# A Strassen embedding computed between the pieces of the output projection, kept in DRAM, and a rewritten last stage

## The chip, the cores and the metric

The kernel runs on one core of one Trainium2 chip. The metric is the device time of one execution in microseconds (us), and the time shown for a kernel is the median of several executions. The core has five engines with queues of their own: TensorE (PE, the matmuls), VectorE (DVE), ScalarE (ACT), GpSimd (POOL) and SyncE (SP). Transfers between DRAM and the on-chip memory SBUF are issued from the SP queue and from the POOL queue, each in its own order; an issue that has to wait holds back every later issue of its queue. Matmuls write to banks of 128 x 512 f32.

## What is computed

```python
hn  = rmsnorm(x, norm_g)                       # x: 512 x 2048, f32
y   = swa_mixer(hn, w_in, w_out, sinks, rel_bias)   # sliding-window attention,
                                               # ends with (out * silu(gate)) @ w_out
x   = x + y
emb = p @ ple_proj                             # 512 x 256 by 256 x 2048
g   = sigmoid(rmsnorm(x, ple_norm) @ ple_gate) # 2048 x 2048 weights
x   = x + emb * g
return rmsnorm(x, final_g)
```

`emb` depends on the inputs `p` and `ple_proj` alone, so it may be computed anywhere before its use in the last line but one.

## The kernel before

**Arithmetic.** Every f32 product is three matmuls in a reduced f32 form: each operand is split into a high part (a cast) and a low part (what the cast left), and `mm3` issues high x high (L126), high x low (L127) and low x high (L128).

**Strassen's scheme.** The two large products with `w_out` and with `ple_gate` (2048 x 2048 each) are computed by Strassen's scheme on quarters. Seven products replace eight. Six of them run in the order 1, 7, 6, 5, 3, 4 (`ORDER_OUT`, `ORDER_PLE`), and one is split once more into seven "small" products. A place in the program is written (p, jj, m): product p, column half jj (0 or 1), piece m (0 to 3). One such piece is a 512 KB block of weights, 128 x 1024, and 12 matmuls of 512 columns into a pair of banks. A small product takes one piece with 6 matmuls at a time; the table `SMALL` says behind which (p, jj, m) each stands.

**The life of a weight piece.** `Pieces` numbers all pieces in the order of use. A piece is loaded by SP (`braw`, L747), some pieces ahead; then ScalarE casts it to `bhi` (L754) and VectorE subtracts that from it to get `blo` (L755). Both go into three buffers each, so the cast of piece n can start only when the last matmul of piece n-3 is done, and the subtraction only when the cast is done. The split of a piece is asked for two pieces ahead of its use. Pieces of the far stretch (from product 6 of `w_out` to the end of that stage) are loaded into eight shared 512 KB rooms (tag "grown"); sums of weights for some products are formed beforehand in DRAM (`sum_weights`) or in these rooms by POOL transfers that add.

**The stages.** Norm, input projection and attention come first (to about 450 us), then the output projection, whose results are added to `x1s` from the banks, then the norm before the gate with transposes (`hT`), then the gate's product, sigmoid and embedding, then the final norm and the stores.

**The embedding before.** It is the direct product: eight "proj" pieces of 512 KB in the gate stage (table `EMBEDS`), split like all pieces, and for each 128 rows x 512 columns six matmuls into a bank of their own (`embed`, bank `e`). The operand p is loaded and split once (`pT` into `pTh`, `pTl`). In the last stage (product 4 of `ple_gate`) the function `block` issues the 24 matmuls of one block of 128 rows and then the block's embedding matmuls; the last block is cut into 288 and 224 columns, `lower` and `upper`. The generator `gated` then takes the sigmoid on ScalarE (L1223), multiplies it by the embedding bank on VectorE (L1225), adds it to x (L1229 on VectorE or by a POOL transfer that adds), and squares for the norm. For the first three of the five last blocks VectorE subtracts the Strassen term kept in `s2` after the matmuls (L1399); for the last two ScalarE writes -`s2` into the bank first and the matmuls add on top.

**What sets the order.** The instructions of PE and SP stand in the order in which they are written, all through. Those of DVE, ACT and POOL are ordered by a scheduler up to the second product of the gate stage, and from there on as they are written too.

## Time and profile before

| | |
|---|---|
| time, median of 3 runs | 789.53 us (789.5 to 790.0) |
| the profiled execution | 789.45 us |
| its span from first to last instruction | 787.7 us |
| mean granted PE clock | 0.996 |
| PE busy | 778.7 us, 99% of the span |
| DVE, ACT, POOL busy | 607.9, 507.0, 139.6 us |
| the last stage, 751.75 to 779.60 us | PE 27.85 of 27.85 us busy |

The 1.75 us between the profiled execution's time and its span lie around the span, where no instruction is recorded. Rows of the timeline give start and length in us; rows of groups give the count, then busy time in us and the mean of one in ns.

### The profile page before, as it was taken

What the parts mean: (1) busy time and instruction counts of PE and PEld (TensorE: products, weight loads), DVE (VectorE), ACT (ScalarE), POOL (GpSimd) and SP (SyncE); (2) the same over time, 40 slices, a digit from 0 to 9 for tenths busy, and PEclk for the clock granted to TensorE, in tenths of its full rate; (3) what the DMA queues carried; (4) which work ended last, traced back from release to release, by engine and by line L of the source; (5) the groups of instructions that cost most, each with busy time, mean ns of one, the idle gap of its engine ahead of it and who ended that gap; (6) DMA issues with size and microseconds to landing.
All of it is one profiled execution on the core that took longest, in us unless ns stands there. A gap on an engine that the chain in (4) does not pass through costs nothing. (4 is left out here: it accounts for less than half of the span.)

```text
span 787.7 us, 11098 instructions
## 1 busy us (share of the span) xinstructions
PE 778.7 (99%) x3726; PEld 651.8 (83%) x3726; DVE 607.9 (77%) x1037; ACT 507.0 (64%) x1064; POOL 139.6 (18%) x258
## 2 busy tenths in 40 slices
PE   9999999999999999999999999999999999999995
PEld 8888888888888888888888888888888888888885
DVE  4547697876877688777777898778879589877896
ACT  6743576666767576766666754456689666656953
POOL 0201423132223323122222200000000022202000
PEclk9999999999999999999999999999999999999998
DMA  9978999999999989999997489667873899979723
GB/s 346 294 206 298 194 274 298 292 280 269 280 275 258 271 232 309 256 289 263 282 258 197 136 320 383 207 209 238 270 265 108 292 290 262 247 239 251 208 86 129
DMA packets 47817, 198.07 MB, mean 251 GB/s; under 512 B 7104, under 2 KB 8128, under 8 KB 42000
## 3 DMA queue, kind: packets, MB, share of 16 engines
q1 hardware_dynamic: 38736, 151.95, 55.7%
q0 software_dynamic: 9024, 45.41, 30.0%
q8 instruction: 29, 0.48, 0.3%
q14 instruction: 28, 0.23, 0.1%
HBM read 189.16 MB, written 71.35 MB: 331 GB/s over the span
## 5 line engine op out<-in xcount | busy, mean ns | idle before, releaser
L755 DVE TENSOR_TENSOR blo<-braw,bhi 128x1024 fp32r<-128x1024 f32 x108 | 131.5, 1222 | 37.3 <-ACT bhi L754 36.4
L754 ACT CAST bhi<-braw 128x1024 fp32r<-128x1024 f32 x108 | 113.4, 1051 | 55.9 <-PE o L128 25.9
L126 PE MATMUL gps<-xh,whi 128*128 128x512 f32 x256 | 100.0, 390 | 0.0
L127 PE MATMUL gps<-xl,whi 128*128 128x512 f32 x256 | 99.9, 390 | 0.0
L128 PE MATMUL gps<-xh,wlo 128*128 128x512 f32 x256 | 99.7, 390 | 0.0
L126 PE MATMUL qps<-xh,whi 128*128 128x512 f32 x224 | 87.8, 392 | 0.0
L127 PE MATMUL qps<-xl,whi 128*128 128x512 f32 x224 | 87.4, 390 | 0.0
L128 PE MATMUL qps<-xh,wlo 128*128 128x512 f32 x224 | 87.3, 390 | 0.0
L110 DVE TENSOR_TENSOR wlo<-wraw,whi 128x1024 fp32r<-128x1024 f32 x60 | 73.5, 1227 | 2.8 <-ACT whi L109 2.7
L570 POOL TENSOR_SCALAR_AFFINE_SELECT own<-r 64x512 fp32r<-64x512 f32 (+1 forms) x48 | 32.5, 677 | 242.9 <-DVE r L560 237.2
L126 PE MATMUL o<-bhi,fho 128*128 128x512 f32 x192 | 74.8, 390 | 0.0
L128 PE MATMUL o<-bhi,flo 128*128 128x512 f32 x192 | 74.8, 389 | 0.0
L127 PE MATMUL o<-blo,fho 128*128 128x512 f32 x192 | 74.7, 389 | 0.0
L556 ACT CAST r<-pt 128x256 fp32r<-128x256 f32 x64 | 23.9, 374 | 68.8 <-PE pt L551 68.6
L109 ACT CAST whi<-wraw 128x1024 fp32r<-128x1024 f32 x60 | 62.3, 1040 | 4.6 <-issue 4.1
L126 PE MATMUL g<-bhi,fhg 128*128 128x512 f32 x160 | 62.7, 392 | 0.0
L128 PE MATMUL g<-bhi,flg 128*128 128x512 f32 x160 | 62.3, 389 | 0.0
L127 PE MATMUL g<-blo,fhg 128*128 128x512 f32 x160 | 62.3, 389 | 0.0
L128 PEld LDWEIGHTS gps<-xh,wlo 128*128 128x128 f32 x256 | 48.1, 188 | 10.3
L126 PEld LDWEIGHTS gps<-xh,whi 128*128 128x128 f32 x256 | 48.1, 188 | 9.1
L127 PEld LDWEIGHTS gps<-xl,whi 128*128 128x128 f32 x256 | 48.1, 188 | 8.8
L560 DVE TENSOR_TENSOR r<-pt,r 128x256 fp32r<-128x256 f32 x56 | 23.7, 424 | 41.0 <-ACT r L556 40.3
(244 smaller groups left out, 1789.3 us busy)
## 6 DMA issues: line engine op xcount, KB each, us to landing
wraw<-in_w_gate_in SPq DMA_DIRECT2D x32, 512.0 KB, 8.3
w_out<-in_w_out POOLq DMA_DIRECT2D x32, 512.0 KB, 9.0
braw<-w_out SPq DMA_DIRECT2D x32, 512.0 KB, 4.8
wraw<-in_w_q SPq DMA_DIRECT2D x28, 512.0 KB, 6.6
braw<-in_w_out SPq DMA_DIRECT2D x22, 512.0 KB, 4.1
braw<-in_ple_gate SPq DMA_DIRECT2D x22, 512.0 KB, 5.4
xw<-in_first SPq DMA_DIRECT2D x14, 640.5 KB, 6.7
w_out<-in_w_out SPq DMA_DIRECT2D x16, 512.0 KB, 10.2
```

Source lines behind the costliest of these rows:

```text
L109: nc.scalar.copy(hi, raw)
L110: nc.vector.tensor_sub(lo, raw, hi.bitcast(F32))
L126: nc.tensor.matmul(ps, sh, mh, start=first, stop=False, skip_group_check=more)
L127: nc.tensor.matmul(ps, sh, ml, start=False, stop=False, skip_group_check=more)
L128: nc.tensor.matmul(ps, sl, mh, start=False, stop=last, skip_group_check=more)
L556: nc.scalar.copy(rh, src)
L560: nc.vector.tensor_sub(rl, src, rh.bitcast(F32))
L570: nc.gpsimd.affine_select(out=flat(own), in_=flat(r).bitcast(F32), pattern=[[0, 8], [sign, HB]], compare_op=ALU.is_ge, fill=0.0, base=-HB ...
L754: nc.scalar.copy(hi, raw)
L755: nc.vector.tensor_sub(lo, raw, hi.bitcast(F32))
```

## The change

The embedding leaves the gate stage. A new class `Embedding` computes it by Strassen's scheme: for each column half, seven products of quarter blocks (two blocks of 128 rows each, three matmuls each: 42 matmuls, all 512 wide), in nine slots between pieces of the output projection (`EMBED_AT`). The sums of quarters of p are made on chip (`make_forms`), the sums of quarters of `ple_proj` with 256 KB loads, two VectorE additions and two POOL transfers that add for each column half, in the rooms of s1 and s7; in each slot the sum is split like a weight piece (the pieces of kind "emb" are numbered with the others). Results come out of the banks by ScalarE copies or VectorE additions, partial sums are put back into banks by ScalarE, and eight 512 KB stores on the POOL queue keep the embedding in DRAM (`embeds`). The gate stage reads them back by eight 512 KB loads on SP in place of the "proj" pieces; `gated` multiplies by that tile instead of a bank.

The small products of `w_out` start later, in product 3 instead of product 5, and (4, 1, 0) has two of them in a row. Pieces of the far stretch are loaded at most 5 ahead instead of 6, and a growing sum is asked for 3 pieces after its last use instead of 6.

In the last stage all five blocks start from a bank that ScalarE has filled with -`s2` (`open_bank`), so no subtraction (old L1399) is left. More additions to x go by POOL transfers, the square of block (3, 1)'s lower part is taken on ScalarE, and some rows are scaled on ScalarE (`rows_by_root`), with the gain multiplied on VectorE.

```diff
     SMALL = {
         "w_out": {
-            (5, 0): {1: [1], 3: [1]}, (5, 1): {1: [7], 3: [7]}, (3, 0): {1: [6], 3: [6]}, (3, 1): {1: [2], 3: [2]},
-            (4, 0): {0: [5], 1: [5], 2: [4], 3: [4]}, (4, 1): {0: [3], 1: [3]},
+            (3, 0): {1: [1], 2: [1], 3: [7]}, (3, 1): {0: [7], 1: [6], 2: [6], 3: [2]},
+            (4, 0): {0: [2], 1: [5], 2: [5], 3: [4]}, (4, 1): {0: [4, 3], 1: [3]},
         },
...
                 if n is not None:
-                    self.due.append((i + (2 if self.specs[i][0] == "seed" else 6), n))
+                    self.due.append((i + (2 if self.specs[i][0] == "seed" else 3), n))
                     self.due.sort()
...
-        def add_embeds(of, j):
-            at["e", of] = len(B.specs)
-            B.add("proj", a["ple_proj"].rearrange("(k p) d -> p k d", p=P)[:, :, j * 512 : (j + 1) * 512])
-
...
+                    if nm == "w_out" and (p, jj, m) in EMBED_AT:
+                        at.setdefault("embed", []).append(len(B.specs))
+                        B.add("emb", None)
...
-                for of, j in EMBEDS.get((p, jj), ()) if nm == "ple_gate" else ():
-                    add_embeds(of, j)
         return at
     EMBEDS = {
-        (6, 1): [((1, 0), 0)], (5, 0): [((1, 1), 1), ((5, 0), 2)], (5, 1): [((5, 1), 3)],
-        (3, 0): [((3, 0), 2)], (3, 1): [((3, 1), 3)],
+        (6, 1): [(1, 1)], (5, 0): [(5, 0)], (5, 1): [(5, 1)], (3, 0): [(3, 0)], (3, 1): [(3, 1)],
     }
+
+    EMBED_AT = [
+        (6, 1, 0), (6, 1, 1), (6, 1, 3), (5, 0, 0), (5, 0, 2), (5, 0, 3), (5, 1, 1), (5, 1, 2), (3, 0, 0),
+    ]
...
     small_steps = {
-        (6, 1, 2): 1, (5, 0, 0): 7, (5, 0, 2): 7, (5, 1, 0): 6, (5, 1, 2): 6, (3, 0, 2): 2, (3, 1, 0): 5, (3, 1, 2): 5,
-        (3, 1, 3): 4, (4, 0, 1): 3, (4, 0, 3): 3,
+        (5, 1, 2): 1, (5, 1, 3): 7, (3, 0, 1): 7, (3, 0, 2): 6, (3, 0, 3): 6, (3, 1, 0): 2, (3, 1, 1): 5, (3, 1, 2): 5,
+        (4, 0, 0): 4, (4, 0, 1): 3, (4, 0, 2): 3,
+    }
+
+    embeds = {
+        (c, jj): tc.dram_tile([P, 2, 512], F32, name=f"embeds{c}_{jj}") for c in (1, 5, 3, 4) for jj in range(2)
...
+    class Embedding:
...
+            elif step == "sums0":
+                load(b50, src(2, 1, 0))
+                load(b51, src(1, 1, 1))
+                nc.vector.tensor_add(b30, b4, b31)
+                nc.vector.tensor_add(b21, b30, b1)
+                add(b4, src(1, 1, 0))
+                add(b50, b21)
+                B.base.update(zip(self.at, (b1, self.b2, self.b3, b4, b5)))
...
+        def times(self, q, piece, half, banks, first=False):
+            fh, fl = self.forms[q]
+            (bh, bl) = (v[half] for v in piece)
+            for tb in range(2):
+                mm3(banks[tb], fh[:, blk(tb)], fl[:, blk(tb)], bh, bl, first, True, True)
+
+        def bank_pair(self, name, tag):
+            return [bank(f"{name}{self.done}_{tb}", tag) for tb in range(2)]
+
+        def room(self, c):
+            return late.tile([P, 2, 512], F32, tag="grown", name=f"made{c}_{self.done}", bufs=8)
+
+        def keep(self, c, jj, fill, to=None):
+            to = self.room(c) if to is None else to
+            for tb in range(2):
+                fill(to[:, tb], tb)
+            nc.gpsimd.dma_start(embeds[c, jj], to)
+
+        def slot(self):
+
+            k = self.done
+            jj = 0 if k < 5 else 1
+            piece = B.get(self.at[k])
+            if k == 0:
+                self.left()
+            if k in (4, 8):
+                self.times(4, piece, 0, self.Z)
+                self.keep(4, jj if k == 8 else 0, lambda to, tb: nc.scalar.copy(to, self.Z[tb]))
+            if k in (0, 4):
+                self.X = self.bank_pair("eX", "t")
+                self.times(1, piece, 1 if k else 0, self.X, True)
+                self.O = self.bank_pair("eO", "o")
+                for tb in range(2):
+                    nc.scalar.mul(self.O[tb], self.X[tb], -1.0)
+            elif k in (1, 5):
+                self.times(2, piece, 0, self.O)
+                self.times(6, piece, 1, self.X)
+                self.keep(1, jj, lambda to, tb: nc.scalar.copy(to, self.O[tb]))
+                self.Y = self.bank_pair("eY", "o")
+                for tb in range(2):
+                    nc.scalar.copy(self.Y[tb], self.X[tb])
+            elif k in (2, 6):
+                self.times(7, piece, 0, self.Y)
+                self.times(3, piece, 1, self.X)
+                for tb in range(2):
+                    nc.scalar.copy(self.left_of[:, tb], self.Y[tb])
+                self.upper = self.room(3)
+                for tb in range(2):
+                    nc.scalar.copy(self.upper[:, tb], self.X[tb])
+            elif k in (3, 7):
+                self.W = self.bank_pair("eW", "o")
+                self.times(5, piece, 0, self.W, True)
+                self.keep(5, jj, lambda to, tb: nc.vector.tensor_add(to, self.W[tb], self.left_of[:, tb]))
+                self.keep(3, jj, lambda to, tb: nc.vector.tensor_add(to, self.W[tb], to), self.upper)
+                self.Z = self.bank_pair("eZ", "o")
+                for tb in range(2):
+                    nc.scalar.mul(self.Z[tb], self.left_of[:, tb], -1.0)
+            self.done += 1
+
...
+    embedding = Embedding(at_out["embed"])
+    embed_steps = {
+        (7, 1, 2): "p", (6, 0, 0): "load0", (6, 0, 1): "forms", (6, 0, 2): "sums0", (6, 1, 1): "load1", (6, 1, 2): "load2",
+        (5, 0, 0): "load3", (5, 0, 1): "sums1",
     }
...
+                if (p, jj, m) in EMBED_AT:
+                    embedding.slot()
...
-    pT = wpool.tile([P, WE], F32, tag="wraw", name="pT").rearrange("p (k t) -> p k t", k=2)
-    nc.sync.dma_start(pT, a["pT"])
-    nc.scalar.copy(pTh, pT)
-    nc.vector.tensor_sub(pTl, pT, pTh.bitcast(F32))
     done = {t: 0 for t in range(NB)}
-    def embed(t, w, tag, c=slice(0, 512)):
-        e_ps = bank(f"e{t}_{done[t]}", tag)
-        for k in range(2):
-            mm3(e_ps[:, c], pTh[:, k, blk(t)], pTl[:, k, blk(t)], w[0][k][:, c], w[1][k][:, c], k == 0, k == 1)
-        return e_ps
-
-    def gated(t, j, zin, z, e_ps, c=slice(0, 512), share=1.0):
+    embed_of = {}
+
+    def load_embeds(c, jj):
+        t = embed_of[c, jj] = late.tile([P, 2, 512], F32, tag="e", name=f"e{c}_{jj}", bufs=2)
+        nc.sync.dma_start(t, embeds[c, jj])
+
+    def embeds_for(of, which):
+        return {t: embed_of[of, which][:, t % 2] for t in ((2, 3) if of == 5 else (0, 1))}
+
+    embed_loads = {
+        (6, 0, 3): (1, 0), (6, 1, 1): (1, 1), (5, 0, 1): (5, 0), (5, 1, 1): (5, 1), (3, 0, 1): (3, 0), (3, 1, 1): (3, 1),
+        (3, 1, 3): (4, 0),
+    }
+
+    def gated(t, j, zin, z, e, c=slice(0, 512), share=1.0):
...
-        nc.vector.tensor_mul(z, e_ps[:, c], z)
-        if (t >= 2) == (j >= 2):
+        nc.vector.tensor_mul(z, e[:, c], z)
+        if (t >= 2) == (j >= 2) or (t, j) in ((0, 2), (1, 2), (2, 0)):
+            if t < 2 and j < 2:
+                yield
...
+    opened = {}
+
+    def open_bank(jj, tb, tag, c=slice(0, 512)):
+
+        ps = opened[jj, tb, c.start] = bank(f"open{jj}_{tb}_{c.start}", tag)
+        nc.scalar.mul(ps[:, c], s2[:, jj, tb, c], -1.0)
+
+    opens = {
+        (3, 1, 0): (0, 0, "t"), (3, 1, 1): (1, 0, "t"), (3, 1, 2): (0, 1, "o"), (3, 1, 3): (1, 1, "o", lower),
+    }
...
-    def block(jj, tb, tag, e_tag, c=slice(0, 512), share=1.0, opened_ps=None):
-
-        ps = bank(f"last{jj}_{tb}_{c.start}", tag) if opened_ps is None else opened_ps
+    def block(jj, tb, c=slice(0, 512), share=1.0):
+
+        ps = opened[jj, tb, c.start]
         for k in range(8):
             fh, fl = f[k // 2]
             bh, bl = B.made[at_ple[4, jj][k // 2]]
             mm3(
                 ps[:, c], fh[:, k % 2, blk(tb)], fl[:, k % 2, blk(tb)], bh[k % 2][:, c], bl[k % 2][:, c],
-                k == 0 and opened_ps is None, k == 7, opened_ps is not None,
+                False, k == 7, True,
             )
-        e_ps = embed(2 + tb, w[jj], e_tag, c)
-        z = s2[:, jj, tb, c]
-
-        def opened():
-            if opened_ps is not None:
-                return gated(2 + tb, jj, ps[:, c], z, e_ps, c, share)
-            nc.vector.tensor_sub(z, ps[:, c], z)
-            return gated(2 + tb, jj, z, z, e_ps, c, share)
-
-        return opened
-
-
+        return gated(2 + tb, jj, ps[:, c], s2[:, jj, tb, c], embed_of[4, jj][:, tb], c, share)
...
+    def rows_by_root(t, js):
+        for j in js:
+            nc.scalar.mul(x1[j][:, t, :], x1[j][:, t, :], yn2[:, t : t + 1])
+            store(t, j)
...
-    g = block(0, 1, "p", "o")()
     run(root)
-    next(g)
-    upper_ps = opened_bank(1, 1, "s", upper)
+    for j in (2, 3):
+        by_gain(3, j)
     for j in range(2):
         row(2, j, yn2[:, 2:])
         store(2, j)
-    for j in (2, 3):
-        nc.scalar.mul(x1[j][:, 2, :], x1[j][:, 2, :], yn2[:, 2:])
-        store(2, j)
+    g = block(0, 1)
     next(g)
+    next(g)
+    rows_by_root(2, (2, 3))
     run(g)
     base, yn = (const.tile([P, 1], F32, name=f"{v}_3") for v in ("base", "yn"))
-    g = block(1, 1, "p", "t", lower, opened_ps=lower_ps)()
+    g = block(1, 1, lower)
+    next(g)
     next(g)
     by_gain(3, 0)
-    next(g)
     run(g)
     n = done[3]
-    last = block(1, 1, "s", "o", upper, 1.0 / D, upper_ps)()
+    last = block(1, 1, upper, 1.0 / D)
     next(last)
     nc.vector.tensor_reduce(base, ssq3[:, 3, :n], axis=AX.X, op=ALU.add)
```

TensorE, the end of its program. `open` is the bank of the last 224 columns, `last`/`low` the high and low part of the last weight pieces, `fhg`/`flg` those of the activations, `e` the embedding's bank. Before:

```order
L128 MATMUL open_1_288_7793<-last_7641,flg_10_7475 128x224
L126 MATMUL open_1_288_7793<-last_7641,fhg_11_7501 128x224
L127 MATMUL open_1_288_7793<-low_7645,fhg_11_7501 128x224
L128 MATMUL open_1_288_7793<-last_7641,flg_11_7502 128x224
L126 MATMUL e_4_7868<-bhi_7617,pTh 128x224
L127 MATMUL e_4_7868<-blo_7618,pTh 128x224
L128 MATMUL e_4_7868<-bhi_7617,pTl 128x224
```

And TensorE around the embedding's second slot, behind piece (6, 1, 1) of the output projection, after the change (`o` are that product's banks, `eO` and `eX` the embedding's, `p_high`, `p_low` and `p_rest` parts of p):

```order
L127 MATMUL o_1_1_5134<-blo_5506,fho_01_5280 128x512
L128 MATMUL o_1_1_5134<-bhi_5505,flo_01_5281 128x512
L126 MATMUL eO_0_5539<-bhi_5526,p_high 128x512
L127 MATMUL eO_0_5539<-blo_5527,p_high 128x512
L128 MATMUL eO_0_5539<-bhi_5526,p_low 128x512
L126 MATMUL eO_1_5540<-bhi_5526,p_high 128x512
L127 MATMUL eO_1_5540<-blo_5527,p_high 128x512
L128 MATMUL eO_1_5540<-bhi_5526,p_low 128x512
```

The matmuls of the bank `e` are gone from the gate stage, and 84 others stand in the nine slots; in all PE's program is 18 rows shorter.

VectorE around the subtraction that makes the second form of the transposed activations (`hT`, 128 x 4 x 256) while the last pieces of the output projection are split. Before, the splits there are of pieces 58 and 59:

```order
L755 TENSOR_TENSOR blo_6206<-braw_6108,bhi_6205 128x1024
L1054 TENSOR_TENSOR x1s<-smallo_6154,x1s 128x512
L755 TENSOR_TENSOR blo_6218<-braw_6120,bhi_6217 128x1024
L863 SCALAR_TENSOR_TENSOR flg_01_6275<-hT_6050,fhg_01_6274 128x512
L855 TENSOR_TENSOR hT_6050<-hT_6050 128x4x256
L755 TENSOR_TENSOR blo_6240<-braw_6155,bhi_6239 128x1024
```

After, those of pieces 65, 66 and 67:

```order
L1049 TENSOR_TENSOR x1s<-o_0_1_6244,x1s 128x512
L756 TENSOR_TENSOR blo_6425<-braw_6339,bhi_6424 128x1024
L756 TENSOR_TENSOR blo_6439<-braw_6375,bhi_6438 128x1024
L861 SCALAR_TENSOR_TENSOR flg_01_6508<-hT_6265,fhg_01_6507 128x512
L853 TENSOR_TENSOR hT_6265<-hT_6265 128x4x256
L756 TENSOR_TENSOR blo_6463<-braw_6387,bhi_6462 128x1024
```

ScalarE there after the change, from the cast of piece 65 (`bhi_6424`) to that of piece 66, with four evacuations of transposes between:

```order
L755 CAST bhi_6424<-braw_6339 128x1024
L1036 ACTIVATE hT_6265<-tp_0_6407,pn 128x256 x2
L1036 ACTIVATE hT_6316<-tp_0_6414,pn 128x256 x2
L755 CAST bhi_6438<-braw_6375 128x1024
L1019 ACTIVATE s_5037,ssq_5034<-x1s 128x512
```

On VectorE the rows are the same as before, but the piece whose low part stands behind the subtraction is now piece (4, 1, 1), whose two predecessors on PE are small products of 6 matmuls; before, one of 6 and one of 12 stood there.

GpSimd's queue after the change, from the second set of weight sums (`s`, in the rooms of s1 and s7) to the norm before the gate (`rstd`); `made` is a 512 KB room that holds one quarter column of the embedding:

```order
L1240 DMA embeds_0_5043<-made_2_5646 128x1024
L1188 DMA s_5038<-in_ple_proj 128x512
L1189 DMA s_5038<-s_5036 128x512
L1240 DMA embeds_0_5045<-made_4_5753 128x1024
L1240 DMA embeds_1_5040<-made_5_5804 128x1024
L1240 DMA embeds_1_5042<-made_7_5913 128x1024
L1240 DMA embeds_1_5044<-made_6_5878 128x1024
L1240 DMA embeds_1_5046<-made_8_5986 128x1024
L1361 TENSOR_TENSOR rstd_6603<-ms_r_6714,power 128x4
```

The eight stores are new, and each `made` is one of the eight shared 512 KB rooms into which SP loads weight pieces: SP loads piece 39 into the room that the store `embeds5_0` reads (the second of the eight, `made_3`), and piece 47 into that of `embeds5_1` (`made_7`), and its queue stands in order.

200 lines of the change are left out of this document (141 added, 59 removed).

## The prediction

> **What bounds the kernel now.** I read the page's busy shares first, then PE's waits, then the busy time by stretch. All times are us.
>
> ```profile
> PE 778.7 (99%) x3726; PEld 651.8 (83%) x3726; DVE 607.9 (77%) x1037; ACT 507.0 (64%) x1064; POOL 139.6 (18%) x258
> PE warm_ps L141 <- PEq L1537: 0.9, 1, 0.9
> core 0: us, PE busy (x) PEld busy (x) DVE busy (x) ACT busy (x) POOL busy (x), PEclk, DMA share, GB/s
> 494.10:570.20 76.10, 76.10 (x337) 63.04 (x336) 60.16 (x70) 45.19 (x60) 0.00 (x0) 1.00 0.71 228
> 587.50:604.90 17.40, 17.40 (x88) 14.54 (x87) 16.63 (x19) 17.11 (x32) 0.00 (x0) 1.00 0.24 84
> 751.75:779.60 27.85, 27.85 (x151) 24.15 (x149) 25.58 (x44) 13.45 (x28) 1.91 (x3) 1.00 0.35 114
> ```
>
> The only wait of PE in the whole list is 0.9 at the start, and in each stretch that the change touches PE is busy from end to end at full granted clock. So a matmul taken away is worth its whole step, as long as nobody else becomes late. Two stretches have little room for that: from 587.5 to 604.9 ScalarE (17.11) and VectorE (16.63) are nearly as full as PE (17.40), and in the last stage VectorE has 25.58 of 27.85.
>
> **Part 1, matmuls removed and added.**
>
> ```profile
> L126 PE MATMUL e<-bhi,pTh 128*128 128x512 f32 (+2 forms) x34 | 12.8, 377 | 0.0
> 721.83 0.39 PE L126 MATMUL e<-bhi,pTh 128*128 128x512 f32 x1
> 724.55 0.39 PE L126 MATMUL g<-bhi,fhg 128*128 128x512 f32 x1
> 775.30 0.29 PE L126 MATMUL e<-bhi,pTh 128*128 128x288 f32 x1
> 776.09 0.26 PE L126 MATMUL open<-last,fhg 128*128 128x224 f32 x1
> 778.76 0.27 PE L126 MATMUL e<-bhi,pTh 128*128 128x224 f32 x1
> 779.32 0.27 PE L128 MATMUL e<-bhi,pTl 128*128 128x224 f32 x1
> ```
>
> The mean of 377 ns is no price, because matmuls overlap: twelve 512-wide ones start between 721.83 and 724.55, so one step is 2.72/12 = 0.2267. The embedding has 3 x 34 = 102 matmuls: 90 full (20.40), six of 288 columns (776.09 - 775.30 = 0.79) and six of 224, whose starts span 0.56, so 0.56 x 6/5 = 0.67. That is 21.86. The new embedding has 84 full ones: 19.04. The small products stay at 14. PE is left with **2.82** less.
>
> **Part 2, the end.** The last six matmuls hid the sigmoid.
>
> ```profile
> 778.65 0.28 PE L128 MATMUL open<-last,flg 128*128 128x224 f32 x1
> 779.02 0.45 ACT L1223 ACTIVATE s<-open,rstd 128x224 f32<-128x224 f32 x1 [2.49 <-PE open L128]
> 779.70 0.39 DVE L1225 TENSOR_TENSOR s<-e,s 128x224 f32<-128x224 f32 x1 [0.72 <-PE e L128]
> ```
>
> Measured from the last `open` matmul, the sigmoid starts 0.37 later and lasts 0.45; with a handover of 0.04 between engines (the cast and subtraction of part 3) VectorE could multiply at 778.65 + 0.37 + 0.45 + 0.04 = 779.51 instead of 779.70. Of the 0.67 only 0.19 remains, so **0.48** is given back. All behind that multiplication is the same chain as before.
>
> **Part 3, the split of a piece behind two small products.**
>
> ```profile
> 722.73 1.03 ACT L754 CAST bhi<-braw 128x1024 fp32r<-128x1024 f32 x1
> 723.80 1.23 DVE L755 TENSOR_TENSOR blo<-braw,bhi 128x1024 fp32r<-128x1024 f32 x1 [0.77 <-ACT bhi L754]
> 588.68 1.56 ACT L1041 ACTIVATE hT<-tp,pn 128x256 f32<-128x256 f32 x4
> 587.38 0.69 DVE L863 SCALAR_TENSOR_TENSOR flg<-hT,fhg 128x512 fp32r<-128x512 f32 x1
> 635.09 1.22 DVE L855 TENSOR_TENSOR hT<-hT,hT 128x1024 f32<-128x1024 f32 x1
> 636.23 0.68 DVE L1091 TENSOR_TENSOR small_sums_g<-hT,small_sums_g 128x512 f32<-128x512 f32 x1
> 593.69 1.23 DVE L855 TENSOR_TENSOR hT<-hT 128x1024 f32<-128x1024 f32 x1
> ```
>
> In (4, 1, 0) PE now runs piece 64 (12 matmuls, 2.72), then the small pieces 65 and 66 (1.36 each), then piece 67. With three buffers the cast of piece 66 may start when 63 is done, 2.72 ahead of the two small products, that of 67 when 64 is done. Between the casts of 65 and 66 four hT evacuations stand in ScalarE's program (1.56). Taking the start of the two small products as zero: piece 62 is done 2.72 + 1.36 and eight transposes of 128 columns (8 x 0.2267/4 = 0.45) earlier, at -4.53; cast 65 ends at -3.45, the evacuations at -1.9, and cast 66, free from -2.72, at -0.85. VectorE, in the order shown with the change, ends the low part of 66 at 0.41, `flg` at 1.10, the hT subtraction at 2.33 and the low part of 67 at 3.55, or 3.3 if adjoining records overlap by 0.08 each, as at 635.09 + 1.22 and 636.23. PE needs that operand in the second matmul of piece 67, at 2.72 + 0.23 = 2.95. It is 0.35 to 0.6 late: I take **0.4**, nearer the overlapping records. The bounds: if the evacuations end before -2.72, all is 0.8 earlier and nothing late; if a square (0.6) that the order has one cast later is still in front, 1.0 to 1.2 is lost. Behind the waiting matmul the whole of PE stands. Before, 18 matmuls (4.08) stood between the same two points instead of 12.
>
> **Part 4, the stores on POOL and the rooms that they hold.** SP loads piece 47 into the room of `embeds5_1`, so its queue stops until that store has landed.
>
> ```profile
> braw<-small_w_out SPq DMA_DIRECT2D x8, 512.0 KB, 4.1
> out<-x1s SPq DMA_DIRECT2D x14, 256.0 KB, 2.8
> out<-x1s SPq DMA_DIRECT2D x1, 512.0 KB, 3.5
> x1s<-in_x POOLq DMA_DIRECT2D x1, 1024.0 KB, 5.5
> grown<-in_ple_gate POOLq DMA_DIRECT2D x16, 512.0 KB, 8.1
> w_out<-in_w_out POOLq DMA_DIRECT2D x32, 512.0 KB, 9.0
> ```
>
> From the end of the slot's matmuls to the end of piece 44, when cast 47 may start, PE has 60 matmuls, 13.6. VectorE's additions and what stands among them take some 2.3 of it, and the load of the piece 4.1, which leaves 7.2 for the store's landing. Pieces 45 and 46 (18 matmuls, 4.08) cover up to 2.0 more of a late cast if ScalarE is otherwise on time; since its queue is busy I count 0.5 of it: free up to 7.7. No 512 KB store on POOL is in the trace. Below stands the store of the same size on SP, 3.5, above the transfers that add or copy in DRAM, 8.1 and 9.0. The nearest is the plain 1 MB transfer on the same queue, 5.5. I take 3.5 to 5.5, so **0**; at 8.1 it costs 0.4, at 9.0 1.3. The first store's room (`embeds5_0`, piece 39) has the same shape. The Trainium skill, "DMA: Bandwidth & Descriptors", section "Anatomy of one DMA — SWDGE (gpsimd) path", fits such transfers by 2.0 us plus bytes over 436e3; by it 524,288 bytes would land in an estimated 3.2, and the sum would be the same, while the 8.1 row shows that not every transfer of that queue keeps to it.
>
> **Part 5, more work on ScalarE and VectorE in the output projection.**
>
> ```profile
> 592.29 0.64 ACT L862 ACTIVATE fhg<-hT 128x512 fp32r<-128x512 f32 x1
> L1270 ACT COPY s<-g 128x512 f32<-128x512 f32 x2 | 1.2, 589 | 2.0 <-PE g L128 2.0
> L1399 DVE TENSOR_TENSOR s<-last,s 128x512 f32<-128x512 f32 x3 | 2.1, 684 | 0.0
> ```
>
> ScalarE gets 28 copies or fills of 512 columns (0.59, 16.5), casts of the nine sums (five of 1024 columns 1.05, four of 512 columns 0.64, so 7.8) and four casts for the forms of p (some 2.3): 26.6. VectorE gets 12 additions of 512 columns (0.68, 8.2), nine low parts (5 x 1.22 + 4 x 0.69 = 8.9) and for the forms four low parts and four differences of 256 columns (at most 0.69 and 0.4 each, 4.2): 21.3. The stretch 494.1 to 570.2 grows on PE from 76.1 by 19.04 less one small pair that moves out (1.36) to 93.8; ScalarE then has about 71, VectorE about 80 of it. Nothing is full on average, so **0**; a bank filled late by ScalarE costs its delay. After a slot the fill has the 12 matmuls of the next piece, 2.72, to hide in. The full stretch behind 587.5 loses the split of pT (1.05 and 1.22) and gets a small product (PE 1.36 and the same split): it stays as tight as it is, which is where part 3 comes from.
>
> **Part 6, the gate stage and the last stage.** Eight 512 KB loads take the place of eight on the same queue, and eight splits go: **0**. In the last stage PE keeps 3 x 24 x 0.2267 + 24 x 0.131 + 24 x 0.112 = 22.2 (the 288-wide step is 0.79/6). VectorE loses three subtractions (2.1), two splits (2.5) and two additions that POOL takes (1.4), some 6 of 25.6, so it needs 19.6 of 22.2. The tightest place is between the two blocks of the last 512 columns:
>
> ```profile
> 776.05 0.48 ACT L1223 ACTIVATE s<-open,rstd 128x288 f32<-128x288 f32 x1
> 776.79 0.45 DVE L1225 TENSOR_TENSOR s<-e,s 128x288 f32<-128x288 f32 x1
> 777.27 0.46 DVE L1229 TENSOR_TENSOR x1s<-x1s,s 128x288 f32<-128x288 f32 x1
> 778.27 0.16 DVE L1469 TENSOR_REDUCE base<-ssq 128x1 f32<-128x4 f32 x1
> 778.53 0.45 DVE L1472 TENSOR_TENSOR x1s<-x1s,fg 128x288 f32<-128x288 f32 x1
> ```
>
> From the last lower matmul: sigmoid 0.37 to 0.85, product to 1.34, addition to 1.80, then the square, now on ScalarE, with its read-out (0.48 + 0.19, as an estimate from the sigmoid's row) to 2.5 while VectorE multiplies a gain (0.69), then sums 0.16 and 0.15 and the product by the gain 0.45, to 3.3. The upper product can start 24 x 0.112 + 0.86 = 3.55 after the same matmul. **0**, with 0.25 to spare, and what is missing is lost if it is not so.
>
> **Sum.** 789.45 (this execution) - 2.82 + 0.48 + 0.40 = 787.51. The execution lies 0.08 below the median of the runs, so 787.6.
>
> **Rivals.**
>
> *No stall behind the small products* (part 3 at its lower bound): 787.1 + 0.1 = 787.2. For it speaks that PE waits nowhere in the trace, also where a pair of small products stands; against it, how thin that is:
>
> ```profile
> 644.31 0.39 PE L126 MATMUL smallg<-bhi,small_ahg 128*128 128x512 f32 x1
> 645.75 1.22 DVE L755 TENSOR_TENSOR blo<-grown,bhi 128x1024 fp32r<-128x1024 f32 x1
> 647.25 0.39 PE L127 MATMUL g<-blo,fhg 128*128 128x512 f32 x1
> ```
>
> There the low part ends at 646.97, 0.28 ahead of its use, without a subtraction between.
>
> *Several thin places give way*: stores as slow as 8.1 (0.4) and two or three splits or bank fills late by 0.2 to 0.5 in the nine slots: 787.6 + 0.4 to 1.6 = 788.0 to 789.2. For it speaks VectorE's rise from 60.16/76.1 = 79% to 85%, against it that ScalarE and VectorE have slack over every ten us.
>
> *The last stage is bound by VectorE*: the lower block's chain is 0.5 to 1 late: 788.1 to 788.6.
>
> *Slower: SP's queue is held by the stores.* The store of `embeds5_1` stands behind other POOL transfers and lands late; piece 47 and all loads behind it on SP start late, PE stops at piece 47. The gain of 1.94 is gone at a landing of 7.7 + 1.9 = 9.6, and the kernel is over 0.2% (1.6) slower from 11.2 on; at 12 it is 787.6 + 4.3 = 791.9. For it speaks the row of 9.0; against it, DMA share 0.71 in that stretch, and plain stores at 2.8 to 3.5. With a stop of over 3 the Trainium skill, "TensorE: Matmul & The Clock Gate", "Part 1: The HAM clock gate", would add a period at half clock, since a window of about 3.4 us idle closes the gate; no run here shows it, the granted clock is 1.00 in all rows above.
>
> That PE does not lose matmuls is excluded by its program, which is 18 rows shorter.
>
> **How the numbers follow.** Forecast 787.6, 0.42; no stall 0.17; several thin places 0.17; VectorE in the last stage 0.10; slower 0.14. A measurement of this kernel tells about 0.2%, 1.6, from no change: faster means under 787.95. Forecast, no stall and a sixth of the thin places lie there, 0.62; the rest of those and the last stage are within, 0.24; slower 0.14. The range reaches from part 3's lower bound with 0.4 for rounding of the steps, 786.8, to past the thin places, 789.8; only the slower case lies outside.
>
> **What would show it.** Right: PE rows 102 less and 84 more, span about 785.8, one wait of some 0.4 at piece (4, 1, 1) on a low part by VectorE, the last multiplication 0.8 to 0.9 behind the last matmul's start. Wrong: PE waits in the nine slots on banks filled by ScalarE or on `blo` (thin places), on a piece whose load follows a store (stores landing beyond 7.7), or VectorE without idle time in the last stage and the last matmuls waiting for it.

## The result, and the profile after

| | before | after |
|---|---|---|
| time, median of 7 runs each | 789.87 us (789.5 to 790.47) | 787.26 us (787.21 to 787.94) |
| ratio after to before | | 0.997, 95% interval 0.9958 to 0.9981 |
| the profiled execution | 789.45 us | 787.21 us |
| its span | 787.7 us | 785.5 us |
| first matmul of the output projection to the end of the span (the *stretch*) | 787.74 - 450.55 = 337.19 us | 785.50 - 450.54 = 334.96 us |
| last matmul's start to the end of the span | 787.74 - 779.32 = 8.42 us | 785.50 - 776.70 = 8.80 us |

The kernel became faster by 2.61 us between the medians and by 2.24 us between the two profiled executions; 787.6 was predicted, in a range of 786.8 to 789.8. (Of the 2.61, 0.34 comes from the kernel before: its median is 789.87 here and was 789.53 in the runs that the prediction started from.) The stretch is what the change touches, and it is the better ruler: in a second set of the changed kernel it was 334.96 again, while the medians move by some tenths; in the profiled executions below it starts anywhere between 450.49 and 451.43 us.

The profile page's busy shares and PE's list of waits, of the kernel after:

```profile
PE 776.1 (99%) x3708; PEld 649.3 (83%) x3708; DVE 611.1 (78%) x1049; ACT 526.0 (67%) x1105; POOL 149.9 (19%) x273
PE warm_ps L141 <- PEq L1720: 0.8, 1, 0.8
```

18 matmuls fewer and still no listed wait of PE behind the start. The busy time by stretch of the kernel after (PE, PEld, DVE, ACT, POOL, then granted clock, DMA share, GB/s): the output projection with the slots, the second half of its last product (what 587.50 to 604.90 was before, with one small product more), and the last stage:

```profile
494.10:587.40 93.30, 93.30 (x413) 77.28 (x412) 75.97 (x95) 66.27 (x98) 7.86 (x12) 1.00 0.80 274
605.20:624.10 18.90, 18.90 (x94) 15.55 (x93) 17.30 (x20) 17.39 (x32) 0.00 (x0) 1.00 0.26 103
749.00:777.30 28.30, 27.97 (x146) 24.01 (x144) 24.87 (x41) 19.93 (x43) 5.03 (x7) 1.00 0.60 177
```

PE is full in all three. The 0.33 us that it lacks in the third lie behind its last matmul (776.70 + 0.27 to 777.30). ScalarE and VectorE stand at 71% and 81% in the slots.

The timeline of the end, PE, ScalarE, VectorE:

```profile
776.70 0.27 PE L128 MATMUL open<-last,flg 128*128 128x224 f32 x1
777.07 0.45 ACT L1387 ACTIVATE s<-open,rstd 128x224 f32<-128x224 f32 x1 [0.61 <-PE open L128]
777.55 0.39 DVE L1389 TENSOR_TENSOR s<-e,s 128x224 f32<-128x224 f32 x1 [0.35 <-ACT s L1387]
```

The last multiplication starts 0.85 behind the last matmul's start and now waits for the sigmoid; before it was 1.05, for PE.

The timeline around piece 67, PE, then ScalarE (the cast of piece 66), then VectorE (the low part of 66, `flg`, the subtraction of hT, and the low part of 67, in one row with that of the next piece):

```profile
612.88 0.39 PE L126 MATMUL o<-bhi,fho 128*128 128x512 f32 x1
613.16 0.50 PE L127 MATMUL o<-blo,fho 128*128 128x512 f32 x1
613.50 0.40 PE L128 MATMUL o<-bhi,flo 128*128 128x512 f32 x1
...
607.78 1.06 ACT L755 CAST bhi<-braw 128x1024 fp32r<-128x1024 f32 x1
...
608.88 1.23 DVE L756 TENSOR_TENSOR blo<-braw,bhi 128x1024 fp32r<-128x1024 f32 x1 [0.81 <-ACT bhi L755]
610.02 0.69 DVE L861 SCALAR_TENSOR_TENSOR flg<-hT,fhg 128x512 fp32r<-128x512 f32 x1
610.74 1.22 DVE L853 TENSOR_TENSOR hT<-hT 128x1024 f32<-128x1024 f32 x1
611.89 2.35 DVE L756 TENSOR_TENSOR blo<-braw,bhi 128x1024 fp32r<-128x1024 f32 x2
```

Steps between starts are 0.28 and 0.34 instead of 0.227: the matmul that reads the low part of piece 67 comes 0.05 late, and the one behind it another 0.11, 0.16 in all. The list of waits does not show it, since PE's records overlap the gap; it is found only by the starts.

The stores and the loads of the embedding, and what held SP's queue between 545 and 580 us (in the first two rows the last number is the median landing; in the third stand the wait in all, the times, and the longest):

```profile
embeds<-made POOLq DMA_DIRECT2D x8, 512.0 KB, 3.7
e<-embeds SPq DMA_DIRECT2D x8, 512.0 KB, 7.3
...
SPq L747 <- DMA embeds<-made: 14.0, 3, 6.2
```

SP did stop at rooms that the stores held, for 14.0 us in three places, and no step between PE's starts is longer there. Of the 6.2 us in front of piece 47 only the last 2.9 are the landing of the store; until 555.15 the store was not issued yet.

### The profile page after: what moved, and what is told of

The parts are those of the page before. It is cut to its first block, busy times and chain, and to the rows that moved or that the text cites. A ratio compares the mean times of both kernels' runs of the same rounds, so it can differ in the third digit from the quotient of the medians.

```text
span 785.5 us, 11165 instructions
## 1 busy us (share of the span) xinstructions
PE 776.1 (99%) x3708; PEld 649.3 (83%) x3708; DVE 611.1 (78%) x1049; ACT 526.0 (67%) x1105; POOL 149.9 (19%) x273
## 4 chain that ended last, share of the span: by engine, by line
PE 98%; issue 1%; DVE 0%; POOL 0%; POOLq 0%; DVEq 0%
PE gps L126 7%; PE gps L127 7%; PE gps L128 7%; PE qps L126 7%; PE qps L127 7%; PE qps L128 7%; PE o L127 6%; PE o L128 6%; PE o L126 6%; PE g L128 5%; PE g L127 5%; PE g L126 5%; PE s L485 2%; PE vps L290 2%; PE pt L551 2%; PE o L598 2%
## 5 line engine op out<-in xcount | busy, mean ns | idle before, releaser
L756 DVE TENSOR_TENSOR blo<-braw,bhi 128x1024 fp32r<-128x1024 f32 x100 | 122.1, 1223 | 30.6 <-ACT bhi L755 29.8
L755 ACT CAST bhi<-braw 128x1024 fp32r<-128x1024 f32 x100 | 105.0, 1051 | 38.9 <-PE o L128 15.5
L128 PEld LDWEIGHTS gps<-xh,wlo 128*128 128x128 f32 x256 | 48.1, 188 | 10.2
L529 ACT ACTIVATE t<-t,sm 128x129 f32<-128x129 f32 (+1 forms) x128 | 49.6, 389 | 8.8 <-DVE sm L525 7.4
```

Source lines behind the costliest of these rows:

```text
L128: nc.tensor.matmul(ps, sl, mh, start=False, stop=last, skip_group_check=more)
L529: nc.scalar.activation(su, su, AF.Exp, bias=sm[:, u : u + 1], accum_out=sm[:, 2 + u : 3 + u])
L755: nc.scalar.copy(hi[:, :n], raw)
L756: nc.vector.tensor_sub(lo[:, :n], raw, hi[:, :n].bitcast(F32))
```

## The experiments

Each kernel is the changed one with the edit shown. "Stretch" is measured in its profiled execution as above; the changed kernel's is 334.96 us. The times are medians of 5 to 11 runs, beside runs of the kernel before on the same chip (medians 789.6 to 789.73).

| kernel | time, us | ratio to before, 95% interval | stretch, us | against 334.96 |
|---|---|---|---|---|
| e13_after_again | 787.34 | 0.997 (0.9959 to 0.9982) | 334.96 | 0.00 |
| e1_pair_moved | 787.62 | 0.9973 (0.9963 to 0.9983) | 334.82 | -0.14 |
| e2_tail6 | 787.25 | 0.9971 (0.9959 to 0.9982) | 334.97 | +0.01 |
| e12_pair_and_stores | 787.47 | 0.9971 (0.9959 to 0.9982) | 335.05 | +0.09 |
| e6_subtract | 789.21 | 0.9994 (0.9985 to 1.0002) | 336.77 | +1.81 |
| e5_ahead6 | 789.63 | 0.9999 (0.999 to 1.0008) | 336.89 | +1.93 |
| e4_held6 | 790.12 | 1.0004 (0.9995 to 1.0013) | 337.62 | +2.66 |
| e7_slots12 | 790.13 | 1.0006 (0.9997 to 1.0015) | 337.68 | +2.72 |
| e10_due6 | 789.71 | 1.0 (0.9991 to 1.0009) | 337.86 | +2.90 |
| e8_twice | 790.97 | 1.0016 (1.0007 to 1.0025) | 338.51 | +3.55 |
| e3_mid12 | 791.73 | 1.0027 (1.0016 to 1.0038) | 338.83 | +3.87 |
| e9_queue_held | 795.37 | 1.0072 (1.0059 to 1.0084) | 342.15 | +7.19 |

**e13_after_again**, no edit.

> The changed kernel once more, beside the others of this group. Expected: 787.2 to 787.9, the spread of its earlier runs, which comes from before the output projection; the stretch from that projection's first matmul to the end is 334.96 us within 0.05.

Measured 787.34 (787.16 to 788.06) and 334.96: the ruler holds to 0.01 us, the median to some tenths.

**e7_slots12** and **e3_mid12**: what a matmul is worth.

```diff
                 self.times(1, piece, 1 if k else 0, self.X, True)
+                self.times(1, piece, 1 if k else 0, self.X, True)
```

> The changed kernel with the first product of each column half of the embedding issued twice into the same banks (the second start overwrites), twelve matmuls of 512 columns more in the output projection, in banks that are held anyway. Theory A: 12 x 0.2267 = 2.72 us longer from the first matmul of the output projection to the end, no new wait of PE. The run with twelve more in the last stage came out 3.87 longer in that stretch, of which 1.15 was a wait for the spare bank; here that wait cannot be. Rival B (PE has room between the pieces): less than 1 us longer.

```diff
     f = ple_forms.made[4]
+    spare = bank("spare_bank", "p")
+    for k in range(4):
+        bh, bl = B.made[at_ple[4, 0][k % 2]]
+        mm3(spare, f[0][0][:, 0, blk(1)], f[0][1][:, 0, blk(1)], bh[0], bl[0], k == 0, k == 3)
```

> The changed kernel with twelve matmuls of 512 columns more ahead of the last stage's first block, into a bank that nothing reads. Theory A (PE sets the time and a matmul is worth its step of 0.2267 us): 2.72 us longer than the changed kernel, 789.9 to 790.0, as long as the kernel before. Rival B (the gain came from the last stage's new order and VectorE there, PE has room): less than 1 us longer.

Twelve matmuls in banks that are held anyway cost 2.72, the 12 x 0.2267 of the prediction. In the last stage they cost 3.87, because the edit brought a wait of its own, in PE's list of waits:

```profile
PE spare_bank L126 <- ACT s L1387: 0.9, 1, 0.9
```

By the starts the step ahead of the spare bank's first matmul is 1.25 instead of 0.227 and the next 0.34, together 1.13 too long; 2.72 and 1.13 are the 3.87 but for 0.02. Theory A holds in both, and the second, taken alone, would have misled.

**e2_tail6**: the same six matmuls of 224 columns put back at the end.

```diff
     last = block(1, 1, upper, 1.0 / D)
+    spare = bank("spare_bank", "p")
+    for k in range(2):
+        bh, bl = B.made[at_ple[4, 1][k]]
+        mm3(spare[:, upper], f[0][0][:, 0, blk(1)], f[0][1][:, 0, blk(1)], bh[0][:, upper], bl[0][:, upper], k == 0, k == 1)
     next(last)
```

> The changed kernel with six matmuls of 224 columns more behind the last block's, into a bank that nothing reads. Theory A (the last six embedding matmuls before were covered by the sigmoid, so taking them away gained only 0.19 of their 0.67 us): nobody waits for these six, time unchanged, within 0.1 us of the changed kernel, last multiplication still about 0.85 us behind the last block's last matmul start. Rival B (the end follows PE's last matmul): 0.67 us longer.

PE ends later and the multiplication comes no later (timeline, PE and VectorE):

```profile
776.76 0.27 PE L128 MATMUL open<-last,flg 128*128 128x224 f32 x1
777.43 0.28 PE L128 MATMUL spare_bank<-last,flg 128*128 128x224 f32 x1
...
777.61 0.39 DVE L1389 TENSOR_TENSOR s<-e,s 128x224 f32<-128x224 f32 x1 [0.35 <-ACT s L1387]
```

777.61 is 0.85 behind the last `open` matmul, as without them; the stretch moved by 0.01. Under the sigmoid six matmuls that nobody reads are free.

**e1_pair_moved**: the two small products in a row put behind (3, 1, 3).

```diff
-            (3, 0): {1: [1], 2: [1], 3: [7]}, (3, 1): {0: [7], 1: [6], 2: [6], 3: [2]},
-            (4, 0): {0: [2], 1: [5], 2: [5], 3: [4]}, (4, 1): {0: [4, 3], 1: [3]},
+            (3, 0): {1: [1], 2: [1], 3: [7]}, (3, 1): {0: [7], 1: [6], 2: [6], 3: [2, 2]},
+            (4, 0): {0: [5], 1: [5], 2: [4], 3: [4]}, (4, 1): {0: [3], 1: [3]},
```

> The small products of the output projection stand as in the kernel before from product 3's last piece on: (3,1,3) has the two of product 2 in a row, (4,0) one behind each piece, (4,1) one behind each of its first two; the count of matmuls is that of the changed kernel. Theory A (the pair in (4,1,0) makes piece 67's low part late, by 0.16 us in the changed kernel's records): the long step at that piece goes, time 0.16 us below the changed kernel's, 787.0 to 787.2, unless the pair makes the same delay behind (3,1,3), where no subtraction of hT stands between. Rival B (VectorE is full there whatever the order of the small products): the same delay of 0.1 to 0.4 us shows again within 25 us of the end of the output projection, time unchanged or up to 0.3 us longer.

The starts at that piece are regular (timeline, PE):

```profile
613.39 0.39 PE L126 MATMUL o<-bhi,fho 128*128 128x512 f32 x1
613.62 0.39 PE L127 MATMUL o<-blo,fho 128*128 128x512 f32 x1
613.84 0.39 PE L128 MATMUL o<-bhi,flo 128*128 128x512 f32 x1
```

The stretch is 0.14 shorter, and no step above 0.32 is left: theory A. A small delay does show behind the pair's new place, one step of 0.26 at 590.21. The median, 787.62, does not show the gain and misses the 787.0 to 787.2 expected; this kernel's profiled execution began its stretch at 450.97.

**e6_subtract**: three of the five last blocks opened empty, with VectorE's subtraction behind.

```diff
-        (3, 1, 0): (0, 0, "t"), (3, 1, 1): (1, 0, "t"), (3, 1, 2): (0, 1, "o"), (3, 1, 3): (1, 1, "o", lower),
+        (3, 1, 3): (1, 1, "o", lower),
...
+        if full:
+            nc.vector.tensor_sub(z, ps[:, c], z)
+            return gated(2 + tb, jj, z, z, embed_of[4, jj][:, tb], c, share)
```

> The changed kernel with three of the five last blocks started in empty banks again and the Strassen term subtracted by VectorE behind the matmuls, as before (three subtractions of 0.68 us more on VectorE, three fills fewer on ScalarE). Theory A (VectorE needs 19.6 of 22.2 us in the last stage, 21.7 with these): no wait of PE, but the one before the last block lies in the chain that ends with the tail only if VectorE has not caught up, 0 to 0.4 us longer. Rival B (the last stage is what the change gains from): 1 us or more longer.

It came out 1.81 longer, against theory A's 0 to 0.4. PE ended 326.18 behind its stretch's start (326.16 in the changed kernel), so all of it lies behind the last matmul, which starts at 776.93. VectorE's timeline there:

```profile
773.34 0.68 DVE L1578 TENSOR_TENSOR s<-last,s 128x512 f32<-128x512 f32 x1
774.81 0.69 DVE L1389 TENSOR_TENSOR s<-e,s 128x512 f32<-128x512 f32 x1 [0.79 <-ACT s L1387]
775.54 0.69 DVE L1395 TENSOR_TENSOR x1s<-x1s,s 128x512 f32<-128x512 f32 x1
777.40 0.46 DVE L1389 TENSOR_TENSOR s<-e,s 128x288 f32<-128x288 f32 x1 [1.18 <-ACT s L1387]
...
779.59 0.38 DVE L1389 TENSOR_TENSOR s<-e,s 128x224 f32<-128x224 f32 x1
```

The last multiplication is 2.66 behind the last matmul's start instead of 0.85. VectorE was not short of time in sum, it even waited 0.79 and 1.18; the subtraction stands in a series (subtraction, sigmoid, product, addition, square, next sigmoid) that passes between VectorE and ScalarE, and every link now pushes the next. The subtraction at 773.34 itself stands in VectorE's order behind the scaling of other rows. So, in the order that the changed kernel has, the filled banks are what lets the removed matmuls count: without them 1.81 of the 2.23 us gained are gone. Whether another order could do without them was not run.

**e5_ahead6** and **e10_due6**: the two distances.

```diff
-if n not in self.base and n >= self.done and kind not in ("grow", "emb") and (kind == "seed" or n <= i + (5 if far_from <= n < far_to else 4 if i >= far_to else 3)):
+if n not in self.base and n >= self.done and kind not in ("grow", "emb") and (kind == "seed" or n <= i + (6 if far_from <= n < far_to else 4 if i >= far_to else 3)):
...
-                    self.due.append((i + (2 if self.specs[i][0] == "seed" else 3), n))
+                    self.due.append((i + (2 if self.specs[i][0] == "seed" else 6), n))
```

> The changed kernel with the old distances: pieces of the far stretch loaded up to 6 ahead instead of 5, a growing sum asked for 6 pieces after its last use instead of 3. Theory A (loads arrive early enough either way, SP's queue stops at the rooms): same length from the output projection to the end within 0.1 us, the long step at piece 67 still there. Rival B (the smaller distances are what keeps SP from stopping at rooms that the stores still hold): PE waits on pieces 39 to 52, 0.5 to 3 us longer.

Nothing moved in the output projection, as theory A said, but the gate stage lost 1.93, which neither theory had. The second kernel has the lower edit alone, on the *due distance*: how many pieces after its last use a growing sum is asked for.

> The changed kernel with only the due distance of growing sums put back from 3 to 6 pieces, the loads at most 5 ahead. With both distances put back the gate stage was 2.2 us longer: one 512 KB adding transfer issued at 722 us behind two additions to x, landing after 12.5, with the weight loads beside it landing 9 to 10 us after their issue instead of 5 to 6, and PE waiting 1.1 at 741. Theory A (the due distance does it: the transfer is pushed into the stretch where the embedding is read back): the same 1.5 to 2.5 us longer. Rival B (it was the 6 pieces ahead): within 0.2 us of the changed kernel.

It loses as much between the medians (789.71 and 789.63): the due distance does it. Its stretch, 2.90 longer against 1.93, overstates the loss, since the profiled execution is the slowest of its eleven (791.01) and has one wait of PE more. Issues between 715 and 750 us with their median landing, first of e10_due6, then of the changed kernel, and what PE then waits for:

```profile
braw<-in_ple_gate SPq DMA_DIRECT2D x8, 512.0 KB, 9.3
e<-embeds SPq DMA_DIRECT2D x3, 512.0 KB, 11.0
grown<-in_ple_gate POOLq DMA_DIRECT2D x1, 512.0 KB, 12.7
...
PE g L127 <- DVE blo L756: 1.8, 2, 1.1
```

```profile
braw<-in_ple_gate SPq DMA_DIRECT2D x8, 512.0 KB, 5.9
e<-embeds SPq DMA_DIRECT2D x3, 512.0 KB, 7.2
```

The issue of the last adding transfer in POOL's timeline: in the kernel before (distance 6), in the changed kernel (3) and in e10_due6 (6):

```profile
686.68 0.86 POOL L734 DMA_DIRECT2D grown<-in_ple_gate  x1 [1.47 <-DVE blo L755]
705.92 0.87 POOL L734 DMA_DIRECT2D grown<-in_ple_gate  x1 [1.46 <-DVE blo L756]
722.65 1.50 POOL L734 DMA_DIRECT2D grown<-in_ple_gate  x1
```

Behind the gate stage's first matmul (605.58, 624.82 and 625.73) that is 81.1, 81.1 and 96.9. So the new distance did not move the transfer: it kept it in its place. By the program, the distance counts pieces, and the "proj" pieces of that stage no longer count; this reading was not run. With 6, POOL issues the transfer behind two additions to x, into the stretch where the embedding comes back; the loads beside it then land 3 to 4 us later (medians above), and the low parts of pieces come late. What makes landing slower there was not taken apart further.

**e4_held6** and **e9_queue_held**: SP's queue behind a store.

```diff
             nc.gpsimd.dma_start(embeds[c, jj], to)
+            if (c, jj) == (5, 1):
+                for n in range(6):
+                    nc.gpsimd.dma_start(tc.dram_tile([P, 2, 512], F32, name=f"again{n}"), to)
```

> The changed kernel with the store of embeds5_1 followed by six more stores of the same 512 KB room on the POOL queue, into DRAM that nothing reads, so that the room is free for piece 47 only when all seven have landed. One such store landed 3.7 us after its issue (median); at 1.2 to 1.9 us more for each, the last lands 11 to 15 us after the first's issue. Theory A (the room is needed about 7.7 us after the issue, at most 9.2): PE stops at piece 47, and the kernel is 2 to 7 us longer, the landing less 7.7 to 9.2. Rival B (SP has enough pieces ahead, the queue's stop is hidden): within 0.3 us of the changed kernel, no wait of PE at piece 47.

The loss, 2.66, is in theory A's bounds and still no support for it. The load of piece 47 was issued at 559.95, before any of the six stores had landed, so it did not wait for their room; only a later load did, issued at 570.99 (SP's waits):

```profile
SPq L747 <- DMA again<-made: 3.4, 1, 3.4
```

PE waited for the three pieces behind piece 47. Their loads were issued up to 3.7 us later in the stretch than in the changed kernel and landed beside the stores; those of the small products took 10.2 to land (median, 553 to 575 us) against 5.5. So a second kernel holds the queue itself:

```diff
+                if i == 47:
+                    at = embeds[5, 1][:, 0, :256]
+                    for n in range(5):
+                        to = tc.dram_tile([P, 256], F32, name=f"link{n}")
+                        nc.sync.dma_start(to, at)
+                        at = to
                 nc.sync.dma_start(t, src)
```

> The changed kernel with a chain of five 128 KB copies between DRAM rooms ahead of SP's load of piece 47, each waiting for the one before, the first for the store of embeds5_1: the queue is held behind that store for four landings, some 9 us, with little traffic. In the changed kernel that load is issued right at the store's landing (2.9 us after its issue), lands 4.1 later, and lies 4.1 before cast 47 and 5.9 before PE would feel it. Theory A: PE waits at piece 47 and behind it, the loss is the hold less 4.1 to 5.9, 3 to 5 us for a hold of 9. Rival B (six stores more held PE up only by their traffic, SP's queue itself has cover enough): loss under 0.5 us.

The load of piece 47 was issued at 570.47 instead of 558.66 where the store had landed, a hold of 11.81. The stretch lost 7.19. PE's waits, its timeline, and the granted clock in four windows (third number from the end: 1.00, 1.00, 0.50, 1.00):

```profile
PE smallo L126 <- ACT bhi L761: 4.2, 1, 4.2
PE smallo L127 <- DVE blo L762: 0.8, 1, 0.8
...
570.63 0.39 PE L128 MATMUL o<-bhi,flo 128*128 128x512 f32 x1
575.25 0.49 PE L126 MATMUL smallo<-bhi,small_aho 128*128 128x512 f32 x1 [4.23 <-ACT bhi L761]
577.11 0.63 PE L128 MATMUL smallo<-bhi,small_alo 128*128 128x512 f32 x1
577.53 0.63 PE L126 MATMUL smallo<-bhi,small_aho 128*128 128x512 f32 x1
...
571.00:575.20 4.20, 0.02 (x1) 0.00 (x0) 0.75 (x2) 1.77 (x4) 0.00 (x0) 1.00 0.88 293
575.25:576.15 0.90, 0.49 (x1) 0.19 (x1) 0.90 (x1) 0.66 (x3) 0.00 (x0) 1.00 1.08 414
576.20:579.55 3.35, 3.04 (x7) 2.46 (x8) 2.59 (x3) 2.46 (x3) 0.00 (x0) 0.50 1.03 411
579.65:584.00 4.35, 4.35 (x21) 3.56 (x20) 2.40 (x4) 2.52 (x5) 0.00 (x0) 1.00 1.03 415
```

By the starts, PE lost 5.4 in two waits (4.39 and 1.03 over the step of 0.227) and 1.5 in the seven steps behind them, one of 0.59 and six of 0.40 to 0.43, which lie in the stretch at half clock. So the hold was covered for 11.81 - 5.4 = 6.4 us, somewhat more than the 4.1 to 5.9 expected, and theory A holds in kind: the slower rival of the prediction is a real mechanism with a price.

**e8_twice**: ScalarE's embedding copies and fills issued twice.

```diff
+                copy = staticmethod(lambda *v: (nc.scalar.copy(*v), nc.scalar.copy(*v)))
+                mul = staticmethod(lambda *v: (nc.scalar.mul(*v), nc.scalar.mul(*v)))
...
-                    nc.scalar.copy(self.Y[tb], self.X[tb])
+                    twice.copy(self.Y[tb], self.X[tb])
```

> The changed kernel with every copy and fill that ScalarE makes for the embedding issued twice (28 more of 512 columns, 16.5 us more on ScalarE between 494 and 587 us, where it had 66.3 of 93.3). Theory A (on average there is room, 83 of 93, but a cast behind two doubled copies comes late at one or two slots): PE waits at two or three places in the slots, 0.2 to 1.5 us longer in all. Rival B (ScalarE's work in the slots is fully hidden, also twice): same length within 0.1 us. Rival C (the slots stand on the edge): 3 us or more.

Rival C: 3.55 longer, with PE waiting at slots and pieces behind them, in more places than the two or three of theory A. The largest of these places, PE and then ScalarE:

```profile
553.57 0.39 PE L126 MATMUL o<-bhi,fho 128*128 128x512 f32 x1
555.02 0.50 PE L127 MATMUL o<-blo,fho 128*128 128x512 f32 x1 [1.07 <-DVE blo L756]
...
548.04 2.15 ACT L1245 COPY left_of<-eY 128x512 f32<-128x512 f32 x4
549.95 2.19 ACT L1245 COPY made<-eX 128x512 f32<-128x512 f32 x4
551.85 2.18 ACT L755 CAST bhi<-braw 128x1024 fp32r<-128x1024 f32 x2
```

Two casts stand behind the doubled copies of one slot. ScalarE is 78.41 of 96.80 us busy there, 81%, and late all the same: the average hides the bursts. The changed kernel's slots have room, but less than one more set of copies.

**e12_pair_and_stores**: the pair moved as in e1, and the last store of 512 KB made as two.

```diff
-    nc.sync.dma_start(
-        a["out"][3 * P :, 512 : 3 * 512].rearrange("p (j c) -> p j c", j=2), x1s[:, 1:3, 3, :]
-    )
+    store(3, 1)
```

(The scaling of row (3, 2) and `store(3, 2)` move ahead of those of row (3, 3); this part of the edit is not shown.)

> The changed kernel with two edits: the pair of small products stands behind (3,1,3) as in the earlier run, which took the long step at piece 67 away, and the last store of 512 KB is made as two of 256 KB, the first issued as soon as its quarter row is scaled. Expected: 0.13 us less up to the last matmul, and 0.1 to 0.4 less from the last matmul to the end (the last store took 3.57 us to land, those of 256 KB 2.5 to 3.0, but each issue takes SP 0.4): 786.7 to 787.1 where the changed kernel has 787.2. Rival (the four last stores share the same transfer rate): the end moves by less than 0.1.

Up to the last matmul it is 326.01 instead of 326.16, 0.15 less, the pair's part again. Behind it, 9.04 instead of 8.80: the last of four stores is issued at 781.54 instead of 780.96 and lands in 3.37 instead of 3.57. So neither the 0.1 to 0.4 less that was expected nor the rival's change of under 0.1 came: the split store loses 0.24. No version here beats the changed kernel by more than the median can tell; the one with the pair moved is 0.14 shorter by the stretch.

## Why the prediction came out right

**Part 1 (2.82 less on PE).** Right to 0.05. From the stretch's start, the last `open` matmul starts 326.16 instead of 328.10 (778.65 - 450.55), 1.94 earlier; with the 0.67 of the last six, which stood behind it, and the 0.16 lost at piece 67 that is 2.77 without them. e7_slots12 shows the price of a step directly.

**Part 2 (0.48 given back).** Right: the multiplication follows 0.85 behind the last `open` matmul, 0.86 was worked out, 0.20 of the 0.67 remained, and e2_tail6 shows that six matmuls in that place are free when nobody reads their bank.

**Part 3 (0.4 lost at piece 67).** The place and the chain were right, the size was not: 0.16 by the starts, 0.14 by taking it away. The sum had cast 66 start 1.9 ahead of the two small products; it started 2.4 ahead (607.78 against 610.16). About half of this comes from the eight transposes, which the sum put at 0.45. From their first start to that of the next matmul it is 0.79 (PE, then ScalarE's cast of piece 65):

```profile
605.20 1.03 PE L1033 MATMUL tp<-ident,x1s 128*128 128x128 f32 x8
605.99 0.48 PE L126 MATMUL smallo<-bhi,small_aho 128*128 128x512 f32 x1
...
605.39 1.05 ACT L755 CAST bhi<-braw 128x1024 fp32r<-128x1024 f32 x1 [0.38 <-PE o L128]
```

So cast 65 began 4.77 ahead instead of about 4.5. The rest is ScalarE's adjoining records, which overlap by some 0.1 each. From there the chain, low part, `flg`, subtraction, low part, took its time as priced (4.11 from the start of cast 66 to that of the low part of 67, 4.23 in the sum). It left that operand 0.05 late; the other 0.11 is the long step behind a wait, which the sum did not have.

**The sum.** 1.94 was predicted and 2.23 measured by the stretch. The 0.24 of part 3, the 0.05 of part 1 the other way, 0.01 of part 2, and the last store, which ends the span 4.54 behind its issue instead of 4.63 (785.50 - 780.96, 787.74 - 783.11), make up the difference. The rival without a stall gave 787.2, nearer to the time than the forecast, but it is not what happened: the stall is there, at less than half of its price.

**Part 4 (stores free up to 7.7).** The verdict was right; the store that piece 47 waits for landed in 2.91 (555.15 to 558.06), the median of the eight is 3.7, and two of them took 7.6 and 7.9, beyond the 3.5 to 5.5 taken. What was not seen is that the store of `embeds4_1` landed only after 7.89 and held SP from 562.96 to 568.57, in front of piece 52; it was covered too. By e9_queue_held the cover at piece 47 is 6.4 behind the store's landing, so 9.3 behind its issue, at the upper end of 7.2 to 9.2 and not at the 7.7 taken. The run also shows the half clock behind a long stop, for which the prediction had no row.

**Part 5 (slots, 0).** Right, with both engines less loaded than priced (ScalarE 66.27 and VectorE 75.97 of 93.3, against 71 and 80 of 93.8). The tight stretch behind them has 17.39 of ScalarE and 17.30 of VectorE in 18.90, a little looser than before. How far it is from the edge was not read from that sum: e8_twice shows that bursts decide, not the share.

**Part 6 (gate stage and last stage, 0).** Right in the last stage, where VectorE ends its last product by the gain 0.35 ahead of the last multiplication (776.75 + 0.45 and 777.55; 0.25 priced); e6_subtract shows that this hung on the filled banks. In the gate stage the 0 was right for a reason that the prediction did not give: the growing sums' due distance, named in the change and not priced, is worth 2.3 to 2.4 between the medians of e10_due6 or e5_ahead6 and e13_after_again. Loads of the same size on the same queue took 5.9 or 9.3 to land (medians), with no more changed than when POOL issues its adding transfers.

## What to carry to other kernels

Where TensorE is dense, price a change in matmul steps taken from starts, and look at the end apart: matmuls that stand under a wait of the tail were worth nothing here, and the removal of the others counted only because the other engines' series of handovers got shorter too, by the filled banks. Engine shares of 70 to 80% said little here about whether one more burst fits; look for the instruction queued behind the burst and who reads it. Measure changes of a few tenths by the length of the stretch that they touch, and check that an experiment's edit brought no new wait and no other allocation of buffers.

## What was not expected of the hardware

After the stop of 4.4 us in e9_queue_held the granted clock went to half for a while. It is still 1.00 in the 0.9 us behind the end of the stop, 0.50 from 576.20 to 579.55, and 1.00 again from 579.65 on. At 0.50 matmuls of 512 columns stepped at 0.40 to 0.43 us instead of 0.227; with the first, at 0.59, this cost 1.5 us beyond the waits (0.1 of it is the long step told of below). The Trainium skill, "TensorE: Matmul & The Clock Gate", section "Part 1: The HAM clock gate", gives half rate after an idle window of about 3.4 us. This run agrees, with a step 1.9 times as long. After the stops of about 1 us in e3_mid12 and e8_twice no such steps are seen.

Behind the waits of PE at full clock stood one more long step each: 0.28 and then 0.34 at piece 67, 1.25 and 0.34 in e3_mid12, 1.45 and 0.34 in e8_twice. So a wait cost some 0.11 us beyond its own length here, and the one at piece 67, too short for the list of waits, is found only by the starts.
